# A fused GEGLU MLP on one core: gate/up by a 4x2x4 bilinear algorithm from the fourth pass on, and a first pass that loads plain fp32

## The chip, the cores and the metric

The kernel runs on one core of a Trainium2 chip. The metric is device time in microseconds (us) of a whole execution, the median of several runs.

In these kernels PE does matmuls (PEld is its weight load), DVE two-tensor arithmetic, ACT activations, casts and copies out of PSUM (where the matmuls' results land), POOL products of data outside PSUM and the issue of casting DMAs, SP the other DMAs. In the traces each engine works off its instructions in the order of the program, so an instruction that waits holds up all that stand behind it. A "flight" below is the time from the issue of a DMA to the landing of its last byte; an "eviction" takes a result out of PSUM.

## The reference

```python
batch, seq_len, hidden_dim = 8, 1024, 1024          # 8192 rows of x
intermediate_dim = 4 * hidden_dim
gate = x @ w_gate                                    # [8192,1024] @ [1024,4096]
up = x @ w_up
gate = 0.5 * gate * (1 + np.tanh(np.sqrt(2 / np.pi) * (gate + 0.044715 * gate ** 3)))
return ((gate * up) @ w_down).astype(np.float32)     # @ [4096,1024]
```

All inputs are fp32. Both kernels multiply in fp16 and accumulate the products in fp32.

## The kernel before

Eight passes of 1024 rows. In each, a gate/up stage makes `h` (kept on chip), then a down stage multiplies it by w_down. Both stages use a one-level 2x2x2 scheme with 7 products for 8: blocks of the operands are added first, and the products are combined afterwards. Gate/up works in 16 pairs of column tiles, each of 14 products (7 for gate, 7 for up) of four matmuls of 512 columns.

The operand sums of the weights are made on DVE from raw fp16 weights. The raw weights come by a casting DMA from POOL. From the middle of pass 2 on, finished operands, stored in DRAM once, come back instead.

```python
def load_w(p, i):                      # two pairs ahead of use
    for w in range(2):                 # 0 gate, 1 up
        c = ring.tile([P, 4096], FP16, tag="ring", name="wc")      # six of these
        if from_source(p, i):          # p < 2, or the first half of p == 2
            nc.gpsimd.dma_start(out=raw(c), in_=w_v[w][:, :, i * 2 * P : (i + 1) * 2 * P])
        else:
            nc.sync.dma_start(out=c, in_=wop[w][i])
def sums_w(p, i, w):                   # one pair ahead of use, on DVE
    t(s[:, 0], a21, a22, ADD); t(s[:, 1], s[:, 0], a11, SUB)
    t(s[:, 2], a11, a21, SUB); t(s[:, 3], a12, s[:, 1], SUB)
...
    for k in range(KH):                # one product: four matmuls of 512 columns
        nc.tensor.matmul(ps, lhs(k), rhs[:, k, :], start=(first and k == 0), stop=(k == KH - 1), ...)
...
    extra[1].append(lambda i=i: load_w(p, i + 2) if i + 2 < NP else None)
    extra[3].append(lambda i=i: sums_w(p, i + 1, 0))     # behind the third product
    extra[5].append(lambda i=i: sums_w(p, i + 1, 1))
```

`extra[k]` stands in the program behind product k of a pair. Pass 0 also prepares w_down in eight groups: a casting load into one staging place, four sums on DVE, seven stores. x goes through DRAM: a casting copy to fp16, then four DMA transposes a pass.

## Time and profile before

| | us |
|---|---|
| time, median of 3 (2418.62 to 2420.49) | 2419.24 |
| gate/up + down of a steady pass | 193.4 + 96.7 |
| start: first product that finds all it needs | 54.8 |
| pass 0's down stage starts | 278.0 |
| gate/up of passes 1 and 2 | 193.4, 206.9 |

The table comes from the start times of the matmuls: a steady gate/up stage is 896 matmuls x 215.8 ns, with no gap. Whatever pass 0 to 2 take beyond 193.4 is loss. Two more lines, from the timeline of the start, tell what the change's second part is aimed at (start us, length, engine, line, what, and in brackets the idle time and what ended it):

```profile
14.76 33.98 SPq L91 DMA_TRANSPOSE x_b<-x_half  x4
...
54.78 1.89 PE L241 MATMUL ps_b<-x_t,wc 128*128 128x512 f16 x4 [21.45 <-DVE wc L142]
```

The four transposes hold SP's queue until 49 us, and the matmuls stand from 33 to 55 us for sums that need them.

### The profile page before, as it was taken

How to read it: one execution, taken by the hardware profiler on the slowest of the kernel's cores; microseconds unless marked ns; L12 is line 12 of the kernel's file. 1: busy time of each engine (PE TensorE's matmuls, PEld its weight loads, DVE VectorE, ACT ScalarE, POOL GpSimd, SP SyncE). 2: the span in 40 equal slices, each digit the busy share in tenths (PEclk: the TensorE clock that was granted, in tenths of full speed). 3: DMA queues.
4: the chain of work that ended last, by engine and by line, in shares of the span. 5: the costliest groups of instructions: out<-in, count | busy, mean ns of one | idle time of the engine just before them, and what ended most of it. 6: DMA issues, size and time to landing. Idle time of an engine off the chain costs nothing.

```text
span 2422.5 us, 27727 instructions
## 1 busy us (share of the span) xinstructions
PE 2335.6 (96%) x10752; PEld 1055.0 (44%) x10752; DVE 1027.3 (42%) x1504; ACT 830.1 (34%) x1410; POOL 577.8 (24%) x484
## 2 busy tenths in 40 slices
PE   1979999999998999999999999999999999999999
PEld 0434444444443444444444444444444444444444
DVE  1757625666163351333513344233522335233350
ACT  0434304442143421444114440244403443044420
POOL 1444203441042310333003330133201332023310
PEclk8989999999998999999999999999999999999999
DMA  9999666998797465544756455564645645554453
GB/s 152 180 204 211 177 195 97 175 262 272 170 272 239 174 218 194 204 185 174 225 194 206 177 186 193 215 209 176 206 166 221 210 175 187 210 197 174 175 187 109
DMA packets 230405, 469.49 MB, mean 194 GB/s; under 512 B 76160, under 2 KB 164224, under 8 KB 188800
## 3 DMA queue, kind: packets, MB, share of 16 engines
q1 hardware_dynamic: 142208, 400.59, 46.2%
q0 software_dynamic: 88064, 67.12, 19.1%
q8 instruction: 84, 1.38, 0.2%
q14 instruction: 49, 0.40, 0.1%
HBM read 436.21 MB, written 98.57 MB: 221 GB/s over the span
## 4 chain that ended last, share of the span: by engine, by line
PE 90%; DMA 7%; SPq 1%; DVE 1%; issue 0%; POOL 0%; ACT 0%; POOLq 0%; DVEq 0%; ACTq 0%
PE ps_a L241 33%; PE ps_da L375 18%; PE ps_b L241 17%; PE ps_db L375 9%; PE ps_c L241 8%; PE ps_dc L375 5%; DMA h_s<-in_w_down_dram 3%; DMA wd_ops<-h_s 2%; SPq L91 1%; DMA wc<-in_w_up_dram 1%; DMA x_half<-in_x_dram 1%; DMA x_b<-x_half 0%; SPq L189 0%; DVE t L255 0%; DVE h_s L170 0%
## 5 line engine op out<-in xcount | busy, mean ns | idle before, releaser
L241 PEld LDWEIGHTS <-wc 128*128 128x128 f16 x7168 | 704.3, 98 | 940.6 <-issue 63.3
L261 POOL TENSOR_TENSOR h_a<-t 128x512 f16<-128x512 f32 x384 | 496.7, 1294 | 1510.8 <-DVE t L255 1414.5
L241 PE MATMUL ps_a<-x_t,wc 128*128 128x512 f16 x3072 | 728.3, 380 | 12.4 <-ACT t L248 12.4
L248 ACT ACTIVATE t<-ps_a 128x512 f32<-128x512 f32 x768 | 458.0, 597 | 499.1 <-PE ps_a L241 499.1
L253 DVE TENSOR_TENSOR t<-ps_b,t 128x512 f32<-128x512 f32 x256 | 176.9, 691 | 691.6 <-ACT t L248 671.3
L375 PEld LDWEIGHTS <-h_a 128*128 128x128 f16 x3072 | 300.6, 98 | 362.5
L258 ACT ACTIVATE t<-t 128x512 f32<-128x512 f32 x384 | 240.9, 627 | 326.0 <-DVE t L253 325.3
L375 PE MATMUL ps_da<-dc,h_a 128*128 128x512 f16 x1536 | 335.4, 379 | 0.0
L347 ACT ACTIVATE o<-ps_da 128x512 f32<-128x512 f32 x128 | 76.4, 597 | 698.0 <-PE ps_da L375 698.0
L241 PE MATMUL ps_b<-x_t,wc 128*128 128x512 f16 x1024 | 264.5, 381 | 21.5 <-DVE wc L142 21.5
L241 PE MATMUL ps_a<-x_b,wc 128*128 128x512 f16 x1024 | 246.8, 385 | 29.8 <-DMA x_b<-x_half 29.8
L241 PE MATMUL ps_b<-x_b,wc 128*128 128x512 f16 x1024 | 246.2, 384 | 19.7 <-DVE t L253 19.7
L241 PE MATMUL ps_c<-x_b,wc 128*128 128x512 f16 x1024 | 262.8, 379 | 0.0
L375 PE MATMUL ps_db<-dc,h_a 128*128 128x512 f16 x1024 | 223.6, 379 | 0.0
L255 DVE SCALAR_TENSOR_TENSOR t<-ps_b,t 128x512 f32<-128x512 f32 x256 | 177.0, 691 | 40.1 <-PE ps_b L241 21.8
L350 DVE SCALAR_TENSOR_TENSOR o<-ps_db,o 128x512 f32<-128x512 f32 x64 | 44.3, 692 | 328.2 <-ACT o L347 244.9
L264 DVE SCALAR_TENSOR_TENSOR h_a<-ps_a,t 128x512 f16<-128x512 f32 x128 | 88.5, 691 | 83.3 <-PE ps_a L241 80.0
L375 PE MATMUL ps_dc<-dc,h_a 128*128 128x512 f16 x512 | 111.8, 379 | 0.0
L375 PE MATMUL ps_da<-dc,h_s 128*128 128x512 f16 x512 | 111.8, 379 | 0.0
L354 DVE TENSOR_TENSOR h_a<-h_a,h_a 128x2048 f16<-128x2048 f16 x96 | 110.2, 1214 | 0.0
L269 ACT ACTIVATE t<-ps_a 128x512 f32<-128x512 f32 x128 | 76.3, 596 | 65.6 <-PE ps_a L241 65.6
L255 DVE SCALAR_TENSOR_TENSOR t<-ps_c,t 128x512 f32<-128x512 f32 x128 | 88.4, 691 | 11.9
(26 smaller groups left out, 516.7 us busy)
## 6 DMA issues: line engine op xcount, KB each, us to landing
wc<-w_ops SPq DMA_DIRECT2D x176, 1024.0 KB, 6.4
dc<-wd_ops SPq DMA_DIRECT2D x112, 1024.0 KB, 6.5
out_dram<-o SPq DMA_DIRECT2D x128, 256.0 KB, 2.4
w_ops<-wc SPq DMA_DIRECT2D x32, 1024.0 KB, 9.1
wc<-in_w_gate_dram POOLq DMA_DIRECT2D x40, 512.0 KB, 8.0
wc<-in_w_up_dram POOLq DMA_DIRECT2D x40, 512.0 KB, 13.1
x_half<-in_x_dram POOLq DMA_DIRECT2D x8, 2048.0 KB, 15.2
wd_ops<-h_s SPq DMA_DIRECT2D x56, 256.0 KB, 7.8
```

What stands on the lines that cost most here:

```text
L241: nc.tensor.matmul(ps, lhs(k), rhs[:, k, :], start=(first and k == 0), stop=(k == KH - 1), skip_group_check=True,)
L248: nc.scalar.activation(tl((n, w)), bank["a", w], COPY, scale=1.0 if w == 0 else HSC)
L253: nc.vector.tensor_tensor(o, bank[b, w], o, ADD)
L255: nc.vector.scalar_tensor_tensor(o, bank[b, w], HSC, o, MUL, ADD)
L258: nc.scalar.activation(t[n, 0], t[n, 0], GELU)
L261: nc.gpsimd.tensor_tensor(hq[h][:, i, :], t[n, 1], t[n, 0], MUL)
L264: nc.vector.scalar_tensor_tensor(hq["a12"][:, i, :], bank["a", 1], HSC, t["gl21"], MUL, MUL)
L269: nc.scalar.activation(tl("gl21"), bank["a", 0], GELU)
L347: nc.scalar.activation(tl((n, g)), bank["a", g], COPY, scale=OSC)
L350: nc.vector.scalar_tensor_tensor(t[n, g], bank[b, g], OSC, t[n, g], MUL, ADD)
L354: nc.vector.tensor_tensor(hq[o][:, s, :], hq[a][:, s, :], hq[b][:, s, :], op)
L375: nc.tensor.matmul(bank[b, g], lhs[:, j, g * P : (g + 1) * P], dc[:, n, :], start=(first and j == 0), stop=(j == NP - 1), skip_group_check ...
```

## The change

Its intent is twofold. From pass 3 on ("fast" passes) gate/up works in 8 quads: four column tiles against four quarters of the rows, 26 products instead of 32. It needs 24 operands of each quad's weights, which DVE and ACT make in passes 1 and 2 and SP stores. And pass 0 starts on plain fp32 loads: x is cast on DVE and transposed on PE, and the weights are cast on ACT from two staging places. The diff cut to its core:

```diff
@@ fast passes: one product is eight matmuls of 256 columns
+            for w in range(2):
+                for k in range(KH):
+                    nc.tensor.matmul(
+                        ps_all[:, bank[c], w * MQ : (w + 1) * MQ], lhs[:, w, k], rhs[:, k],
+                        start=(first and w == 0 and k == 0), stop=(k == KH - 1), ...)
+                load_a(q * NCH + j + 12)              # 512 KB of operands, a quad ahead
@@ raw weights of passes 1 and 2: a quad at a time, two buffers
+    def raw(p, q):
+        o = 8192 * ((q + p) % 2)
+        return rg[:, o : o + 8192].rearrange("p (w k n) -> p w k n", w=2, k=2 * KH)
+            elif e == 0:                              # e: first or second pair of the quad
+                at(1, load_raw, p, q + 1)             # POOL, casting, 2 x 1 MB
+            for n, k in enumerate(ks):                # ks = 3, 5, 7, 9
+                at(k, sum_w, p, i + 1, n)
@@ operands of the fast passes, made in passes 1 and 2
+            if FAST - 2 <= p < FAST:
+                for j, n in enumerate(entries_of(p - FAST + 2)):
+                    if j // 6 == e:
+                        at(2 * (j % 6) + 2, make_entry, p, q, n)      # one sum and one store
@@ pass 0: plain loads into two staging places, casts on ACT
+                if e == 0:
+                    at(5 if first else 1, load_stage, q + 1, 0, 0, 0)
+                    at(5 if first else 1, load_stage, q + 1, 1, 0, 1)
+                    at(10, cast_stage, q + 1, 0, 0, 0)
+                    at(12, cast_stage, q + 1, 1, 0, 1)
+                    at(11, load_stage, q + 1, 0, 1, 0)
+                    at(13, load_stage, q + 1, 1, 1, 1)
+                else:
+                    at(6, cast_stage, q + 1, 0, 1, 0)
+                    at(8, cast_stage, q + 1, 1, 1, 1)
... (cut: tables of the algorithm, the evictions' schedule, the start, x's sums in the down stage)
```

## The prediction

> **What bounds the kernel now.** I read the page first, then the PE's own waits, then the chain of waits in order of time, then a table of stages, then the timeline of the start.
>
> ```profile
> span 2422.5 us, 27727 instructions
> PE 2335.6 (96%) x10752; PEld 1055.0 (44%) x10752; DVE 1027.3 (42%) x1504; ACT 830.1 (34%) x1410; POOL 577.8 (24%) x484
> PE 90%; DMA 7%; SPq 1%; DVE 1%; issue 0%; POOL 0%; ACT 0%; POOLq 0%; DVEq 0%; ACTq 0%
> ```
> The matmul engine works 96% of the span and is 90% of the chain that ended last; no other engine is above 42%. From the chain in order of time (start us, length, what):
>
> ```profile
> 1161.88 13.81 PE ps_da L375 x64
> ...
> 1451.96 13.81 PE ps_da L375 x64
> ```
> Both are the first piece of a down stage, in consecutive passes. 64 matmuls take 13.81 us, so 215.8 ns each, and the passes lie 290.08 us apart. A pass has 896 gate/up and 448 down matmuls: 1344 x 0.2158 = 290.0 us. **A steady pass has no idle PE time at all.** All 10752 matmuls are 2320.5 us, so the other 102 us are idle or cold time. The PE's waits:
>
> ```profile
> PE ps_a L241 <- DMA x_b<-x_half: 29.8, 1, 29.8
> PE ps_b L241 <- DVE wc L142: 21.5, 1, 21.5
> PE ps_b L241 <- DVE t L253: 19.7, 4, 10.5
> PE ps_a L241 <- ACT t L248: 12.4, 4, 10.8
> ```
> Placing the loss by when each down stage starts: the first two waits are the start, 51.2 us. Pass 0's down starts at 278.12 where 51.2 + 193.4 would do: 33.5 us lost. The starts of passes 1 and 2 come 290.1 and 303.6 us later: 0 and 13.5 us lost. The end costs 3.5. The stages (us, busy by engine, clock, DMA share, GB/s):
>
> ```profile
> 110.00:165.00 55.00, 41.68 (x180) 18.05 (x179) 29.77 (x57) 18.22 (x32) 18.53 (x17) 0.88 1.14 206
> 375.00:568.00 193.00, 193.00 (x896) 87.46 (x894) 127.08 (x223) 93.97 (x160) 83.58 (x75) 1.00 0.93 199
> 720.00:765.00 45.00, 34.53 (x147) 14.99 (x146) 20.88 (x38) 15.65 (x27) 13.22 (x11) 0.85 1.07 298
> 968.00:1162.00 194.00, 194.00 (x901) 87.91 (x900) 75.25 (x112) 94.13 (x161) 59.68 (x48) 1.00 0.52 190
> ```
> The two stages with idle PE (pass 0, and the first half of pass 2) are those in which the DMA share is over 1. At 0.93 (pass 1) nothing is lost. The steady gate/up runs at 0.52, with DVE busy 39%.
>
> **What the Trainium skill says.** (1) "TensorE: Matmul & The Clock Gate", Back-to-back issue gap: a warm matmul of N columns costs N/2.4 + 2.5 ns, so 262 cycles for 256 columns. The trace agrees at 512: 426.7 ns apart while the clock is at half (512/1.2), 215.8 warm. The same section gives 81 ns for a stream of weight load plus 128-column matmul; no 256-column stream is in this trace. (2) "VectorE: DVE Perf Modes", The TRN2 errata: an fp32 two-tensor operation of N elements takes (N+151)/0.96 ns, 691 at 512; the trace has 691. (3) Same section, ScalarE from SBUF 224+FD cycles at 1.2 GHz: 613 ns for 512; the trace's gelu took 627. I use it for sizes that the trace lacks. (4) "DMA: Bandwidth & Descriptors", Anatomy of one DMA: about 2 us fixed per transfer; no view isolates this.
>
> **The change, part by part.**
>
> *Fast gate/up, passes 3 to 7.* Out: 896 matmuls of 512 columns, 193.4 us. In: 8 quads x 26 products x 2 weights x 4 = 1664 matmuls of 256 columns. Taking the fixed 2.5 ns out of 215.8: 213.3/2 + 2.5 = 109.2 ns each, 181.7 us. Gain 11.7 us a pass, **58 us in five**. (The bare count, 26/32 against 7/8, gives 13.8; the rest goes to the fixed cost, paid twice as often.) It needs the weight load to hide:
>
> ```profile
> L241 PEld LDWEIGHTS <-wc 128*128 128x128 f16 x7168 | 704.3, 98 | 940.6 <-issue 63.3
> L253 DVE TENSOR_TENSOR t<-ps_b,t 128x512 f32<-128x512 f32 x256 | 176.9, 691 | 691.6 <-ACT t L248 671.3
> L248 ACT ACTIVATE t<-ps_a 128x512 f32<-128x512 f32 x768 | 458.0, 597 | 499.1 <-PE ps_a L241 499.1
> L261 POOL TENSOR_TENSOR h_a<-t 128x512 f16<-128x512 f32 x384 | 496.7, 1294 | 1510.8 <-DVE t L255 1414.5
> ```
> A load is 98 ns, 151 at half clock, so about 53 ns scale with the clock and 45 are latency. Its record starts 2 ns after that of the previous matmul, so it has the whole matmul: 98 < 109 fits, narrowly.
>
> Evictions per quad (26 slots of 0.874 us = 22.7 us): DVE 24 x 0.691 + one half-size 0.42 = 17.0 us; ACT 12 x 0.597 + 16 gelus of 256 at 0.40 = 13.6; POOL 15 x about 0.65 = 10. All are below 22.7. Only one slot, the sixteenth, carries two DVE accumulations, so DVE's backlog stays under a slot. Each bank that a product adds to again has at least two whole slots (1.75 us) between the slot of its last reader and that product. I expect no PE wait. DMA: 12 chunks of 512 KB. The packet records give 344 ns for 8 KB and 91 ns for 2 KB, so about 176 for 4 KB: 12 x 128 x 0.176 / 16 = 16.9 us of 22.7, a share of 0.74, under the 0.93 that cost nothing. The sums of x (19 of about 0.68 us, four scalings) lie in the down stage, where DVE is idle by two thirds.
>
> *Start.* 4 MB of x and 4 MB of first weights come as plain fp32 in place of a cast through DRAM and four transposes on the queue. By packets: x 2 x 5.6 us of 16 engines, weights in 1 KB rows (51 ns) 2 x 6.6; the first w_down load (6 us) competes. At the 1.14 share seen above, the first weight half is in at about 18 us, the last bytes near 29. The second half of x's copies on ACT stand behind the last weight casts, so the first product that needs them (P6) starts at about 34 us with 5 products (4.3 us) done: **lost 30 where it was 51, gain 21.**
>
> *Pass 0.* Weight loads, per quad: 2048 packets of 2 KB at 91 ns = 11.6 us, where 4096 casting ones at 65 ns took 16.6, per 24.2 us. The w_down preparation is unchanged at 11.8 us per 18.1. Share 0.69 + 0.65 = 1.34 before, 0.48 + 0.65 = 1.13 after: at the measured ceiling, no longer over it. The casts go to ACT: four of 2048 elements, 1.9 us each, about 9.9 us of ACT per 12.1 us pair. A cast that waits for its load holds up the snaps behind it, and those gate PE. I keep **12 us lost of 33.5, gain 21.**
>
> *Passes 1 and 2.* Each makes half of the 24 operands of each quad: 9 sums on DVE (7.6 us in pass 1, as three negated ones run as two halves of 0.69) plus three copies on ACT. With 14 evictions (9.7 us) and 8 sums of the one-level scheme (5.5), DVE has 22.7 of 24.2 us; back-to-back records overlap by about 0.08 us each, so nearer 20. DMA: 2048 casting packets at about 106 ns (between 65 and 189) = 13.6, stores 8.7, the cast of x 1.2: share 0.97. A quad's load needs some 16 us from issue and its first sum wants it after 12 to 14, so DVE, in order, waits 3 to 5 us and has about that much slack. **16 us lost in both, against 13.5: cost 2.5.**
>
> Sum: matmuls 3 x 193.4 + 5 x 181.7 + 8 x 96.7 = 2262; start 30, pass 0 12, passes 1 and 2 16, end 3.5: **about 2323 us**, 4% faster.
>
> **Rivals.** (a) *Weight loads or issue bound the 256-column stream.* At 120 ns instead of 109 the fast stage takes 199.7 us, longer than the old one: +90 us, 2413, within 2%. For it: 98 of 109 ns leaves little. Against: half of those 98 is latency, and the skill's 81 ns pair. I give it 7%. (b) *DVE becomes the bound in passes 1 and 2*, a new wait for the one removed. For it: about 90% load, an in-order queue with DMA waits, collisions with POOL (some fp16 sums took 0.67 us on average where 0.42 is their floor). If it adds 3 us a quad beyond my 1, +48: 2370. (c) *The startup and pass 0 gain is hidden*: bytes are not fewer, ACT stalls replace DMA stalls. Then 40 us come back: 2363. (d) *Everything hides better* (start 25, passes 0 to 2 lose 10 together): 2300.
>
> **Range and chances.** The 58 us are arithmetic unless (a) holds. The 58 lost around them may be 25 to 105. So 2290 to 2370, centre 2322. Faster by 2% means under 2370.9; missing it needs (a), or (b) and (c) together: faster 0.88, same 0.10, slower 0.02.
>
> **What would show it.** Fast stage: first down matmuls of passes 4 to 7 lie 278.4 us apart, weight-load and matmul starts 109 ns apart, DMA share near 0.75, DVE near 75%. Start: first long run of 512-column products near 34 us. Pass 0: the remaining PE waits name ACT snaps behind casts. Passes 1 and 2: DVE waits for the raw loads, PE waits for DVE, 0 to 2 us a quad. The prediction is wrong if the passes lie 290 us or more apart, or if the down stage of pass 2 starts later than about 872 - 25 us.

## The result, and the profile after

The changed kernel takes **2439.54 us** (2436.95 to 2440.96, 3 runs). The ratio to the kernel before is 1.0081, 95% interval 1.0059 to 1.0104. (Ratios here are the mean time of one kernel's fast runs over that of the other's in the same rounds, so not quite the ratio of the medians quoted.) It is correct.

| us | before | predicted | after |
|---|---|---|---|
| lost at the start | 51.2 | 30 | 31.1 |
| further loss of pass 0 | 33.5 | 12 | 54.4 |
| loss of passes 1 and 2 | 0, 13.5 | 16 together | 43.0, 43.5 |
| gate/up of passes 3 to 7, each | 193.4 | 181.7 | 181.65 |
| whole | 2419 | 2323 | 2440 |

After, pass 0's down stage starts at 278.95, and the start cost 31.1, so 278.95 - 193.4 - 31.1 = 54.4. The gate/up stages of passes 1 and 2 last 236.4 and 236.8.

The page's first lines and its chain:

```profile
span 2437.8 us, 38323 instructions
PE 2317.8 (95%) x14656; PEld 1441.5 (59%) x14656; DVE 1464.8 (60%) x2103; ACT 959.6 (39%) x1822; POOL 683.2 (28%) x797
PE 63%; DMA 5%; DVE 2%; issue 1%; POOL 0%; ACT 0%; POOLq 0%; DVEq 0%; ACTq 0%
```

PE's share hardly moved, from 96% to 95%, which says little: the records of half-sized matmuls last 273 ns on average and start 109 ns apart, so they overlap, and busy time and work done are not the same. The chain in order of time says more. This is its second half (start us, length, what):

```profile
1042.47 181.65 PE ps L646 x1664
1224.12 96.69 PE ps L741 x448
1320.82 181.65 PE ps L646 x1664
1502.47 96.69 PE ps L741 x448
```

From pass 3 to the end every piece is PE, and 181.65 us / 1664 = 109.2 ns a matmul. PE waits for nothing. So the five fast stages gave 58.7 us (5 x (193.39 - 181.65)), and more than that was lost before 1042 us. The same chain inside pass 2:

```profile
768.30 0.94 POOL ring L261
769.24 18.74 DMA ring<-in_w_up_dram
788.13 0.55 issue
788.68 0.68 DVE x_sums L198
789.37 0.60 DVE ring L276
...
798.55 1.04 PE ps L447 x4
799.63 0.95 POOL ring L261
800.59 19.62 DMA ring<-in_w_up_dram
```

Here is a ring that repeats: POOL issues a quad's raw load (L261), 19 us of flight follow, then DVE's sums, a few evictions and products, and then the *next* issue on POOL. From 768.30 to 799.63 it takes 31.3 us; the matmuls of a quad take 24.2. What waits for whom, over the whole kernel (us, times, longest):

```profile
DVE ring L276 <- DMA ring<-in_w_up_dram: 109.3, 14, 10.0
PE ps L447 <- DVE tmp L462: 46.1, 14, 5.2
PE ps L447 <- ACT tmp L458: 34.3, 28, 3.4
```

DVE waits 14 times for a raw load, 7.8 us each. In the table of stages (length, busy time of PE, PEld, DVE, ACT, POOL, clock, DMA share, GB/s) pass 1 and a fast stage read:

```profile
376.00:612.00 236.00, 207.29 (x896) 89.97 (x894) 173.41 (x254) 112.68 (x184) 80.75 (x61) 0.95 0.77 191
1042.00:1224.00 182.00, 182.00 (x1668) 162.95 (x1666) 126.01 (x198) 99.95 (x222) 82.94 (x117) 1.00 0.87 291
```

In pass 1 DVE is busy 73% and the DMA share is 0.77. Neither is used up. The stage that runs without a gap has the *higher* DMA share, 0.87.

The 43 us lost in each of these passes are not all waiting. In pass 2 the starts of the matmuls show 27 us in gaps. The other 16 us come behind the gaps: after each of the six long ones, of 3.5 to 5.6 us from start to start, 7 to 14 of the next 20 matmuls start up to 427 ns apart instead of 215.8 (granted clock 0.5 there, 0.93 over the stage). In pass 1 it is 31 and 12 us. Where the gaps go (third buffer, below) the clock is 1.00.

Pass 0, from the timeline:

```profile
89.92 1.90 ACT L254 CAST ring<-x_sums 128x2048 f16<-128x2048 f32 x1 [6.75 <-DMA x_sums<-in_w_up_dram]
...
94.31 1.89 PE L447 MATMUL ps<-x_sums,ring 128*128 128x512 f16 x4 [5.08 <-DVE ring L276]
```

ACT stands 6.75 us before a cast whose staged load is late. The evictions behind it on ACT are late too, DVE waits for those, and PE stands 5.1 us for a DVE sum.

### The profile page after: what moved, and what is told of

It reads as the page before. It is cut to its first block, busy times and chain, and to the rows that moved or that the text cites. A ratio compares the mean times of both kernels' runs of the same rounds, so it can differ in the third digit from the quotient of the medians.

```text
span 2437.8 us, 38323 instructions
## 1 busy us (share of the span) xinstructions
PE 2317.8 (95%) x14656; PEld 1441.5 (59%) x14656; DVE 1464.8 (60%) x2103; ACT 959.6 (39%) x1822; POOL 683.2 (28%) x797
## 4 chain that ended last, share of the span: by engine, by line
PE 63%; DMA 5%; DVE 2%; issue 1%; POOL 0%; ACT 0%; POOLq 0%; ACTq 0%; DVEq 0%
PE ps L646 37%; PE ps L741 24%; DMA ring<-in_w_up_dram 5%; PE ps L447 2%; DVE tmp L462 1%; DVE ring L276 1%; DVE x_sums L198 0%; POOL ring L261 0%; DVE h_a L477 0%; DVE h_s L198 0%; ACT tmp L458 0%; POOL h_a L469 0%; ACT tmp L467 0%; ACT tmp L697 0%; DVEq L276 0%
## 5 line engine op out<-in xcount | busy, mean ns | idle before, releaser
L646 PEld LDWEIGHTS <-ring 128*128 128x128 f16 x8320 | 814.1, 98 | 95.2
L623 POOL TENSOR_TENSOR h_a<-tmp 128x256 f16<-128x256 f32 x600 | 438.1, 745 | 954.6 <-ACT tmp L611 898.6
L741 PE MATMUL ps<-ring,h_a 128*128 128x512 f16 x3072 | 665.6, 379 | 0.0
L646 PE MATMUL ps<-x_sums,ring 128*128 128x256 f16 x5760 | 654.9, 273 | 0.0
L447 PEld LDWEIGHTS <-ring 128*128 128x128 f16 x2688 | 271.9, 101 | 463.5 <-issue 149.2
L608 DVE TENSOR_TENSOR tmp<-tmp,ps 128x512 f32<-128x512 f32 x600 | 387.0, 684 | 89.1 <-ACT tmp L593 63.0
L447 PE MATMUL ps<-x_sums,ring 128*128 128x512 f16 x1536 | 362.8, 387 | 56.2 <-ACT tmp L458 34.3
L593 ACT COPY tmp<-ps 128x512 f32<-128x512 f32 x480 | 280.7, 586 | 272.1 <-PE ps L646 105.7
L447 PE MATMUL ps<-x_b,ring 128*128 128x512 f16 x1152 | 296.8, 410 | 50.4 <-DVE tmp L462 46.1
L606 DVE TENSOR_TENSOR tmp<-ps,tmp 128x512 f32<-128x512 f32 x320 | 213.6, 688 | 215.3 <-PE ps L646 130.8
L646 PE MATMUL ps<-x_b,ring 128*128 128x256 f16 x2560 | 305.6, 273 | 0.0
L462 DVE TENSOR_TENSOR tmp<-ps,tmp 128x512 f32<-128x512 f32 x288 | 188.6, 682 | 103.6 <-ACT tmp L458 93.8
L458 ACT COPY tmp<-ps 128x512 f32<-128x512 f32 x288 | 163.0, 584 | 88.6 <-PE ps L447 85.1
## 6 DMA issues: line engine op xcount, KB each, us to landing
ring<-in_w_gate_dram POOLq DMA_DIRECT2D x16, 1024.0 KB, 11.3
ring<-in_w_up_dram POOLq DMA_DIRECT2D x16, 1024.0 KB, 17.9
```

Source lines behind the costliest of these rows:

```text
L447: nc.tensor.matmul(ps(b, w), lhs[:, k], rhs[:, k, :], start=(first and k == 0), stop=(k == KH - 1), skip_group_check=True,)
L458: nc.scalar.copy(tl((n, w)), ps("a", w))
L462: nc.vector.tensor_tensor(o, ps(b, w), o, ADD)
L593: nc.scalar.copy(tmp[:, t[o[1]]], ps_all[:, bank[o[2]]])
L606: nc.vector.tensor_tensor(d, b, a, SUB)
L608: nc.vector.tensor_tensor(d, a, b, ADD if o[4] == "add" else SUB)
```

## The experiments

**Theory L** (latency): passes 1 and 2, and pass 0 too, are bound by rings of a buffer's reuse. A load is issued only when the work on the load before it is done, and that work waits in order for that load. The period is flight plus work, whatever the engines' shares. **Rival D**: DVE has too much work in passes 1 and 2. **Rival B**: DMA bandwidth is used up. For pass 0 **rival A**: the 1.9 us casts on ACT hold up the copies out of PSUM.

### A third raw buffer

```diff
-        o = 8192 * ((q + p) % 2)
-        return rg[:, o : o + 8192]...
+        v = (hf["s3"], rg[:, 8192:16384], rg[:, 0:8192])[q % 3]      # passes 1 and 2
-    places = [hf["s3"][:, ...] for j in range(8)] + [xc[:, ...] for j in range(8, len(X_SUMS))]
+    places = [xc[:, ...] for j in range(8, len(X_SUMS))]
-                at(1, load_raw, p, q + 1)
+                at(1, load_raw, p, q + 2)
+                        load_raw(p + 1, 1)           # beside load_raw(p + 1, 0), in the down stage
... (cut: the order in which w_down's chunks use the freed places)
```

> Only passes 1 and 2 are touched: the raw fp16 weights get a third buffer and each load is issued one quad earlier; bytes, sums on DVE, stores and matmuls stay as they are. Gate/up of passes 1 and 2 took 236.4 and 236.8 us where their matmuls need 193.4. Theory L (a loop of latency: a load's issue stands on POOL behind products that wait for sums of the load before, 19 to 20 us in flight + 11.5 us of work = 31 us a quad where the matmuls take 24.2): both stages fall to 193 to 200 us, the kernel to about 2355 to 2365. Rival D (DVE's work is too much in these passes): both stay at 236, kernel 2440. Rival B (DMA bandwidth is used up): both stay at 236 as the bytes are the same.

Measured: 2364.85 us (2363.61 to 2366.36), ratio to before 0.977, interval 0.9755 to 0.9784. Gate/up of passes 1 and 2: 200.2 and 195.4. The stages in its trace:

```profile
378.00:579.00 201.00, 195.44 (x901) 87.94 (x900) 182.06 (x255) 112.44 (x184) 78.00 (x59) 1.00 0.84 215
675.00:871.00 196.00, 195.25 (x900) 87.88 (x899) 176.54 (x245) 112.45 (x184) 77.87 (x59) 1.00 0.86 221
```

The same sums and nearly the same bytes (one quad's load, 2 x 1 MB, moved into the down stage before) fit into 200 and 195 us, with DVE busy 91 and 90% and the DMA share at 0.84 and 0.86. No wait of DVE for a raw load is left in its table of waits. Rivals D and B fall; the cause is the ring. The loads themselves did not get faster (median 17.6 us to landing, where it was 17.9). They only start earlier.

### Both terms of the ring, each by itself

The ring has two terms, flight and work. Three runs shorten one each (the first one less cleanly than meant).

*Less work*: the sums of the operands are left out. Its output is wrong, which doesn't matter for the time.

```diff
-            _, op, a, b = A_SUMS[n - 8]
-            combine(four(v), op, a_node(p, q, a), a_node(p, q, b))
+            o = 8192 * ((q + p) % 2) + 1024 * (n % 8)
+            v = rg[:, o : o + 1024]                  # store raw weights instead
```

> A wrong result on purpose: in passes 1 and 2 the 18 sums a quad are not made, and the store takes 2 KB of the raw weights instead, so DVE loses 6 to 8 us of work a quad while bytes, queues and buffers stay as in the changed kernel. Theory L: the loop gets shorter only by the sums inside it, some 6 of 0.6 us: 27 to 28 us a quad, so the two stages fall from 236 to 210 to 220. Rival D (DVE throughput): they fall to 193 to 197. Rival B: they stay at 236.

Measured (single run): 2408.54 us, the two stages 218.5 and 219.3. With 6 to 8 us of DVE work a quad taken away, 25 us of the 43 lost remain in each. But the edit put something else into the ring: the stores now read the raw buffer itself, so the next load has to wait for them. This run's chain shows it at every turn of pass 2, 2.5 to 3.7 us each time:

```profile
807.66 2.71 DMA w_ops<-ring
810.38 0.94 POOL ring L261
```

So the 25 us that remain are in part the edit's own, and their size says nothing against rival D. What does is that DVE still stands 56 and 58 us in these stages waiting for raw loads; the clean test of rival D is the third buffer.

*Less flight*: no stores beside the loads, but for the first quad. Its output is wrong, which doesn't matter for the time.

```diff
+        if q == 0:
-        nc.sync.dma_start(out=wop[q, e // 2, :, e % 2], in_=v)
+            nc.sync.dma_start(out=wop[q, e // 2, :, e % 2], in_=v)
-in_=wop[q, j]
+in_=wop[0, j]
```

> A wrong result on purpose: of the operands made in passes 1 and 2 only those of the first quad are stored, and the fast passes load these for every quad; DVE's sums, buffers and order stay as in the changed kernel. It measures what the stores add to a raw load's 18 to 19.6 us of flight. Theory L with contention: the flight falls to 14 to 16 us, the loop from 31 to 26 to 28, the two stages from 236 to 200 to 212 us. Rival (the flight is the casting queue's own): it stays at 18 to 19 us and the stages at 230 or more. Theory D (DVE throughput): 236.

Measured (single run): 2377.82 us, the stages 207.6 and 202.1. The two DMA lines below are of the changed kernel, then of this run (last column: median us from issue to landing); the third is this run's wait of DVE:

```profile
ring<-in_w_up_dram POOLq DMA_DIRECT2D x16, 1024.0 KB, 17.9
```

```profile
ring<-in_w_up_dram POOLq DMA_DIRECT2D x16, 1024.0 KB, 12.8
...
DVE ring L276 <- DMA ring<-in_w_up_dram: 41.6, 13, 4.7
```

So of the 18 us in flight of a quad's second raw load, 5 come from the stores of the very operands that the change adds. A packet of these loads takes as long without the stores (103 ns on average, 106 beside them), so the load waits its turn more often and its packets are not slower. The interval between issues falls from 31 to about 26 us. That is the flight's part of the ring, in the size that theory L gives.

*An earlier issue*, still two buffers, one line moved ahead of POOL products that wait for gelu (two by the program, where the text below says three):

```diff
-            elif e == 0:
-                at(1, load_raw, p, q + 1)
+            else:
+                if i == 0:
+                    at(1, load_raw, p, 1)
+            if p > 0 and e == 1:
+                at(12, load_raw, p, q + 2)           # behind the last reader of that buffer
```

> The changed kernel with one line moved: in passes 1 and 2 the raw load of a quad is put on POOL behind the twelfth product of the pair before, as soon as its buffer is free, ahead of three products on POOL that wait for gelu. Still two buffers. Theory L: the work between a landing and the next issue falls from 11.5 to about 8 to 9 us, the loop from 31 to 28, the two stages from 236 to 215 to 222 us. Rival D or B: 236.

Measured (single run): 2404.45 us, the stages 218.2 and 218.3; the issues lie 26.6 to 30.8 us apart. The move alone takes back 18 us a pass, but not the rest: with two buffers the load still stands behind the last product that reads its buffer, and that product stands behind evictions that follow, on DVE, the sums from the load before.

### The plain loads alone

```diff
-    FAST = 3
+    FAST = 8                                         # no fast pass
-            if FAST - 2 <= p < FAST:
+            if False:                                # no operands made
```

> The second part of the change alone: all eight passes on the one-level scheme, raw weights loaded in each pass, no operands made or stored, no fast pass. Pass 0 is as in the changed kernel, so its down stage starts at 279 us and this part by itself brings nothing there. Theory L: without stores a load flies 14 to 16 us and the work between landing and the next issue is about 8 us, 22 to 25 us a quad, so the gate/up stages of passes 1 to 7 take 193 to 200 us; kernel 2410 to 2450. Rival D (one-level sums by themselves are too much beside the raw loads): they take over 205, kernel over 2480.

Measured: 2414.30 us (2411.05 to 2415.24), ratio 0.9967, interval 0.9950 to 0.9983. Pass 0's down stage starts at 282.1 us, and every gate/up stage from pass 1 on takes 193.39 us, with no loss. A raw load is in flight 12.6 us here, and DVE still waits for it 46 times (3.6 us each), which costs nothing: flight and work together stay under 24.2 us. So the same two-buffer ring is harmless by itself, and binds once the operands add to both its terms.

### Pass 0: four staging places

```diff
+    def pieces(q, n): ...         # rows of h that pass 0 fills last serve as two more places
-                    at(11, load_stage, q + 1, 0, 1, 0)          # into the place just cast from
+                        at(11 + 2 * w, load_deep, q + 2, w, 0, w)   # a quad ahead
+                            at(7 + 2 * w, load_deep, q + 2, w, 1, 2 + w)
```

> Only pass 0 is touched: the staging of fp32 weights for the cast on ACT has four places in place of two (the last quad still two), so a load is issued a quad ahead of its cast. Bytes, casts and their places in ACT's order are the same. Pass 0 loses 54 us behind its start. Theory L (the same loop: a load waits for the cast before it, the cast waits in order on ACT for the load, and the copies out of PSUM behind it hold the matmuls): the loss falls to 10 to 25 us, pass 0's down stage starts at 235 to 250 us instead of 279, kernel about 2400 to 2410. Rival A (the casts' own 1.9 us on ACT hold the copies): the loss stays within 8 us of 54. Rival B (bandwidth): it stays too.

Measured: 2421.05 us (2419.74 to 2422.78), ratio 1.0003, interval 0.9986 to 1.0019. Down of pass 0 starts at 261.8 us; in six runs without an edit to pass 0 it started between 279 and 283. So 17 to 21 us came back where theory L expected 29 to 44, and 37 us of loss remain; all three ranges were missed. Its waits in pass 0:

```profile
PE ps L475 <- ACT tmp L486: 20.9, 13, 5.7
DVE h_s L364 <- DMA h_s<-in_w_down_dram: 13.5, 4, 5.5
...
ACT ring L268 <- DMA x_sums<-in_w_gate_dram: 0.7, 1, 0.7
```

ACT's waits for staged loads, 28 us in the changed kernel's pass 0, are gone (0.7). In their place DVE now waits 13.5 us for w_down's loads, where it waited 4.0 before: one late load had hidden another.

### Both edits

> Both edits together. Theory L: the gains add, 75 to 85 us from passes 1 and 2 and 30 to 45 from pass 0: 2315 to 2335 us, 4% under the kernel before. Rivals D and B: 2440 as it is. If one part falls and not the other, the sum shows it.

Measured: **2343.39 us** (2340.89 to 2347.49), ratio to the kernel before **0.9682**, interval 0.9666 to 0.9699, correct. The edit is the two above together. Passes 1 and 2 take 200.2 and 195.4, and down of pass 0 starts at 263.9. It beats both kernels, but is 8 us slower than the slow end of what was expected, all of it pass 0.

### What is left in pass 0

Undoing one part, with casting loads from POOL again from the second quad on:

```diff
-                    (eight lines of load_stage and cast_stage)
+                    at(5 if first else 1, load_raw, 0, q + 1)
```

> Undoes one part: from the second quad of pass 0 on, the weights come again by casting loads from POOL (2 KB rows, two raw buffers) and ACT makes no casts; the start keeps its plain loads. Theory L: a casting load of 2 MB beside the w_down traffic is in flight 19 us or more against 13.8 from issue to first use, so pass 0 loses as much or more: its down stage starts at 275 to 300 us. Rival A (the casts on ACT are what pass 0 lost by): the loss falls to the 33 of the kernel before, down at 255 to 262 us.

Measured (single run): 2432.11 us, down of pass 0 at 272.2. Neither range held it. But the edit also changed the start, which it was meant to keep. Nothing stands before it on POOL, so the second quad's casting loads are issued at 2.4 us, among the loads of the start, and P6, the first product that needs the second half of x, begins at 46.49 us, where the changed kernel has 35.42:

```profile
2.40 0.91 POOL L261 DMA_DIRECT2D ring<-in_w_gate_dram  x1
...
46.49 1.86 PE L447 MATMUL ps<-x_sums,ring 128*128 128x512 f16 x4 [5.28 <-DVE x_sums L187]
```

The start costs 42.2 us here, and behind it 36.6 us are lost, not 54: close to the 33 of rival A, though DVE waits 21.5 us for w_down's loads. Four staging places, with every cast in its place, came to 37.3. So this run doesn't tell the casts' own time from the late loads that they wait for, since it removes both.

Moving w_down's sums further behind their loads:

```diff
-                    s0 = 21 * n + 2
-                        (0, wd_load, (n,)), (14, wd_sums, (0,)), (15, wd_sums, (1,)), ...
+                    s0 = 24 * n + 2
+                        (0, wd_load, (n,)), (18, wd_sums, (0,)), (19, wd_sums, (1,)), ...
```

> The version with three raw buffers and four staging places (2343 us measured) and one more edit in pass 0: the eight groups of w_down preparation lie 24 products apart in place of 21, and their sums stand on DVE 18 to 21 products behind the load in place of 14 to 17. What is left of pass 0's loss there is 37 to 39 us, in gaps of 2 to 6 us. Theory W (DVE waits in order for the w_down load, 13 us, and the accumulations behind the sums hold PE): the loss falls by 10 to 20 us, the kernel to 2325 to 2335. Rival A (the 1.9 us casts on ACT hold the copies out of PSUM): the loss stays within 5 us, kernel 2340 to 2346.

Measured: 2345.57 us (2345.56 to 2345.60), ratio 0.9687, interval 0.9673 to 0.9702; down of pass 0 at 261.9. No gain. But the edit did not do what it was for: DVE still waits 13.3 us for these loads (12.7 without the edit). It tells nothing about the theories. The next two do.

```diff
+        if q == 0:                                   # w_down loaded once, wrong on purpose
             nc.gpsimd.dma_start(out=hf["s3"][:, 0:4096]..., in_=wd_v[:, 4 * q : 4 * q + 4, :])
```

> A wrong result on purpose, on the version with three raw buffers and four staging places: w_down is loaded once and its first rows are used for all eight groups, so seven of the eight w_down loads of pass 0 (7 x 2 MB read) and every wait of DVE for them go; its sums and stores stay. Pass 0's remaining loss there is 37 to 39 us. Theory W (DVE stands in order behind the w_down load): the loss falls to 20 or less, down of pass 0 at 240 to 245 us instead of 264. Rival A (the 1.9 us casts on ACT hold the copies out of PSUM): it stays at 33 or more.

```diff
-                        at(10 + 2 * w, cast_deep, q + 1, w, 0, w)
+                        for j in range(4):           # four casts of 512 elements
+                            at(s, cast_piece, q + 1, w, 0, w, j)
... (cut: the second half of the rows; three of the four loads move by one product)
```

> On the same version (2343 us), each cast of 2048 elements on ACT becomes four of 512 (0.6 us), spread over products that have no copy out of PSUM behind them. Theory A: no copy waits 1.9 us any more, the remaining loss of pass 0 falls from 37-39 to 25 or less, kernel 2325 to 2332. Theory W: it stays within 5 us, kernel 2340 to 2348.

Measured: with w_down loaded once (single run, 2328.39 us) down of pass 0 starts at 244.8 us, 19 earlier, and 20 us of loss remain. With small casts 2342.21 us (2339.97 to 2343.08), ratio 0.9671, interval 0.9655 to 0.9687, down at 258.1: 6 us earlier than with whole casts, against a spread of 4 us among runs with an unedited pass 0. (The trace with whole casts is of the slowest of that version's four runs, 2347.49 us against a median of 2343.39, so both differences, 19 and 6, may be some 4 us too large.) The kernel's time is within noise of the version with whole casts. In the first of these two runs PE's waits in pass 0 are:

```profile
PE ps L477 <- ACT tmp L488: 15.7, 13, 2.9
PE ps L477 <- DVE x_sums L187: 5.5, 1, 5.5
```

Theory W holds for the larger part. Taking the loads away removes their bytes as well as DVE's waits for them, so how the 19 us split between the two stays open. The last 20 us, mostly PE behind copies on ACT, were not taken apart further.

One more ring can be read from the traces, though no run tests it. w_down has a single staging place, in the kernel before too: a group's load waits for the sums and stores of the group before. From the second to the eighth group the loads are issued 23.5 us apart before and 24.1 after, where 21 products take 18.1; with four staging places for the weights it is 22.4. In part this is effect, as an issue on POOL that stands behind late products comes late. But the chain of the kernel before consists for 51% of the stretch from 54 to 280 us of these loads and stores, in turn:

```profile
96.72 13.71 DMA h_s<-in_w_down_dram
111.39 17.41 DMA wd_ops<-h_s
130.09 8.15 DMA h_s<-in_w_down_dram
```

A second place for w_down was not tried.

## Why the prediction was wrong

Point by point, by its own steps.

- **Fast gate/up: right.** 109.2 ns a matmul and 181.65 us a stage, to the decimal. Weight loads hide (98 ns inside 109), no eviction is late. DMA share was 0.87 for 0.74 (4 KB packets took 191 ns in the records, not 176, and the prefetch of x and of w_down's first chunks falls into the stage, which the 0.74 left out). It cost nothing. Rival (a) fell.
- **Start: right.** The product P6 began at 35.4 us (about 34 foretold), 31.1 us lost for 30.
- **Pass 0: a mechanism was named, its size was wrong.** "A cast that waits for its load holds up the snaps behind it" is what the timeline shows; "I keep 12 us lost of 33.5" should have read 54. The term was taken from the DMA share ("at the measured ceiling, no longer over it"), which was 0.82 over pass 0 in the event. What held it, as far as the runs show: the time from a load's issue to its cast with two places, 17 us of the 54, and w_down's loads, 15 to 19 more, with their bytes and with DVE's waits in order. The last 20 us or so stay open. The 33.5 us of the kernel before were read as DMA share as well ("no longer over it"), where its chain named w_down's loads and stores, which the change left as they were.
- **Passes 1 and 2: the step that failed.** It reads: "A quad's load needs some 16 us from issue and its first sum wants it after 12 to 14, so DVE, in order, waits 3 to 5 us and has about that much slack." The flight was 17.5 to 20.6 us from a quad's first issue to its last byte, and DVE waited 7.8. The larger error is the last clause. Slack on DVE is of no use here: the next load's issue stands on POOL behind products that stand behind these very sums, so a wait delays the next load by as much. The right sum was the period of the ring, about 19.7 + 11.5 = 31.2 us against 24.2, seven microseconds a quad and six quads a pass: 42 us, where 43 were measured. Each run that shortened a term shortened the stages, and the third buffer took out 36 and 41 us. Some 12 and 16 of the 43 are the slower matmuls behind the gaps, a cost of a wait that the prediction's sum has no term for.
- **Rival (b)** had the right stage and "a new wait for the one removed", but named DVE's load as the cause. With the third buffer DVE did the same work in 195 to 200 us, so the load fits. Rival (c), "ACT stalls replace DMA stalls", came true for pass 0, and not alone; the start kept its gain of 20 us.
- **The checks that it named** told it apart in one look: down of pass 2 at 945.6 us was over the limit of 847.

Added up: 2323.4 foretold (its terms before rounding), + 42.4 in pass 0, + 70.5 in passes 1 and 2, + 1.1 at the start, is 2437.4; the profiled run's span was 2437.8.

## What to carry to other kernels

For each buffer that is filled again and again, write down the ring: issue, flight under the traffic of that stage, in-order work until the buffer's next issue. If its period is longer than the compute that it feeds, the stage runs at the ring's pace, whatever the shares of busy time say. Here one more buffer, with the load one turn earlier, brought 36 and 41 us in the two stages; less traffic brought 29 and 35, an earlier issue 18 in each. And a side job that is placed in a stage to be "hidden" can lengthen both terms there, as it did here: flight by its transfers and work by its place in the order.

## What the Trainium skill lacked or had wrong

- "TensorE: Matmul & The Clock Gate", Back-to-back issue gap: N/2.4 + 2.5 ns, which the page gives for the isolated matmul, holds at 256 columns in a stream with a weight load before each matmul (109.2 ns measured, 262 cycles by the page). The same section's sustained figure of 131 ns for 512 columns was not seen: 215.8 ns in every gapless stage of 512-column matmuls, before and after.
- "DMA: Bandwidth & Descriptors", Anatomy of one DMA: its fit, 2.0 us + bytes/436e3, gives by our estimate 4.4 us for 1 MB, or 6.8 for the 2 MB of fp32 that a casting load of 1 MB of fp16 reads. Such a load with 2 KB fp32 rows, issued right behind another like it, landed after 12.6 to 12.8 us without the stores of operands, and after 17.9 beside these stores of 2 KB rows; the first of the two took 8.5 to 8.6, and 11.3. The page has no figure for casting loads of short rows, or for sharing; by the packet records a casting packet of 1 KB out took 106 ns and a plain one of 2 KB 90 ns.
- "VectorE: DVE Perf Modes", The perf-mode tier table, has no row for a scalar-and-two-tensors operation on fp16: 128x512 took 0.68 us at best, no faster than in fp32, where the plain two-tensor sum of twice the size, 128x1024, took 0.68 too. Here a negated sum, made in two halves, costs twice a plain one. I found a time for it on no other page either.
- No page that I found says how to judge a refill ring; the trace showed DVE 73% and DMA 77% busy in a stage that lost 43 us to one.
